# Another order of DRAM rows over the partitions in a contrast kernel

## The chip, the cores and the metric

The kernel runs on one core of a Trainium2 chip. The metric is the device time of one execution in microseconds; the median of three runs before the change is 239.33 us (239.33 to 239.63).

## The reference

The input x is float32, 16 x 3 x 512 x 512: 48 images (16 batches of 3 channels) of 262,144 pixels. Each image is stretched about its own mean, by a factor of 1.5, and clipped to [0, 1]:

```
mean = np.mean(x, axis=(2, 3), keepdims=True)
return np.clip(mean + factor * (x - mean), 0, 1).astype(np.float32)
```

So each output is factor * x plus a number that belongs to its image, (1 - factor) * mean, clipped. The mean needs the whole image before the first pixel of it can be written. 50.3 MB are read and 50.3 MB are written.

## The kernel before

**Tiles.** A row of the kernel is 16,384 consecutive elements (`ROW`, 64 KiB), an image is 16 rows (`ppi`), and a tile is 128 rows, one on each partition: eight whole images (`per_tile`). There are six tiles, 0 to 5 in the code ("tiles two to six" of a count from one are `t` = 1 to 5). `dram(ap, t, c0, c1)` gives the DRAM side of a transfer: rows 128t to 128t + 127 in order, so that row r of the tile stands on partition r, and columns c0 to c1 of each. `load` (L77) and `store` (L80) move such a piece between DRAM and one of three slots of `ring`; both are issued by SyncE, so all transfers go through its one queue in program order.

**Constants.** `blockw`, 128 x 128, holds `wconst` = (1 - factor) / 262,144 where both partitions belong to the same image (the same block of 16) and 0 elsewhere. GpSimd builds it with a memset (L61) and two selects (L63).

**One tile.** `compute(t)` first sums each partition's row. `add` splits it: VectorE reduces the first 4,352 columns (`SUM`, L85), ScalarE copies the other 12,032 in place with an accumulated sum (L89). Two matmuls with the stationary `blockw` (L100) add the two columns of sums over the partitions of an image, scale them by `wconst`, and leave the image's number on each of its partitions in a column of `bias` in PSUM. VectorE then does x * factor + bias (L103) and the clip (L106), both in place, and `store` sends the slot out. Tile 0 is loaded in three pieces, summed in two halves, and stored in two pieces (the first 2,048 columns ahead).

**Order.** The schedule is written out by hand: loads of tiles 0, 1, 2; then `compute` of 0, 1, 2 with their stores; loads of 3, 4, 5; then `compute` of 3, 4, 5. There are 15 transfers: eight loads and seven stores. The load of tile t + 3 waits until the store of tile t has emptied its slot. In the queue, that gives the loads of tiles 0 to 2, the stores of 0 to 2, the loads of 3 to 5, and the stores of 3 to 5.

Of the kernel before, what the change touches and what calls it, by code (L numbers as in the profile page):

```python
# [1 line left out]

# [4 lines left out]


P = 128  # L10
ROW = 16384
HALF = ROW // 2
BUFS = 3
SHORT = 2048
SUM = 4352


@with_exitstack
def kernel(
    ctx: ExitStack,  # L20
    tc: tile.TileContext,
    x: bass.AP,
    factor: float,
    out: bass.AP,
):

    nc = tc.nc
    f32 = mybir.dt.float32  # L30
    Alu = mybir.AluOpType
    Act = mybir.ActivationFunctionType

    B, C, H, W = x.shape
    n_img, n_pix = B * C, H * W
    ppi = n_pix // ROW
    per_tile = P // ppi
    n_tiles = n_img // per_tile
    assert ppi * ROW == n_pix and per_tile * n_tiles == n_img

    factor = float(factor)
    wconst = (1.0 - factor) / float(n_pix)

    x_f = x.rearrange("b c h w -> (b c h w)")
    out_f = out.rearrange("b c h w -> (b c h w)")

    def dram(ap, t, c0=0, c1=ROW):
        return bass.AP(tensor=ap.tensor, offset=t * P * ROW + c0, ap=[[ROW, P], [1, c1 - c0]])

    consts = ctx.enter_context(tc.tile_pool(name="consts", bufs=1))  # L50
    xpool = ctx.enter_context(tc.tile_pool(name="xpool", bufs=1))
    small = ctx.enter_context(tc.tile_pool(name="small", bufs=1))
    psum = ctx.enter_context(tc.tile_pool(name="psum", bufs=1, space=bass.MemoryType.PSUM))


    sums = small.tile([P, 4 * n_tiles], f32, name="sums")
    bias = psum.tile([P, n_tiles], f32, name="bias")

    blockw = consts.tile([P, P], f32, name="blockw")
    blocks = blockw.rearrange("p (a b) -> p a b", b=ppi)  # L60
    nc.gpsimd.memset(blockw, wconst)  # L61
    for base, step in ((0, -ppi), (ppi - 1, ppi)):
        nc.gpsimd.affine_select(  # L63
            out=blocks,
            in_=blocks,
            compare_op=Alu.is_ge,
            fill=0.0,
            base=base,
            pattern=[[step, per_tile], [0, ppi]],
            channel_multiplier=1 if step < 0 else -1,  # L70
        )


    ring = xpool.tile([P, BUFS, ROW], f32, name="ring")

    def load(t, c0=0, c1=ROW):
        nc.sync.dma_start(out=ring[:, t % BUFS, c0:c1], in_=dram(x_f, t, c0, c1))  # L77

    def store(t, c0=0, c1=ROW):
        nc.sync.dma_start(out=dram(out_f, t, c0, c1), in_=ring[:, t % BUFS, c0:c1])  # L80

    def add(t, col, c0, c1, c2):
        xt = ring[:, t % BUFS, :]
        own = sums[:, 4 * t + col : 4 * t + col + 2]
        nc.vector.tensor_reduce(  # L85
            out=own[:, 0:1], in_=xt[:, c0:c1], axis=mybir.AxisListType.X, op=Alu.add
        )
        part = xt[:, c1:c2]
        nc.scalar.activation(out=part, in_=part, func=Act.Copy, accum_out=own[:, 1:2])  # L89
        return [own[:, 1:2], own[:, 0:1]]  # L90

    def compute(t, *cuts):
        xt = ring[:, t % BUFS, :]
        if t == 0:
            parts = add(t, 0, 0, SUM, HALF) + add(t, 2, HALF, HALF + SUM, ROW)
        else:
            parts = add(t, 0, 0, SUM, ROW)
        shift = bias[:, t : t + 1]
        for k, part in enumerate(parts):
            nc.tensor.matmul(shift, blockw, part, start=k == 0, stop=k == len(parts) - 1)  # L100
        for c0, c1 in zip((0, *cuts), (*cuts, ROW)):
            part = xt[:, c0:c1]
            nc.vector.tensor_scalar(  # L103
                out=part, in0=part, scalar1=factor, scalar2=shift, op0=Alu.mult, op1=Alu.add
            )
            nc.vector.tensor_scalar(  # L106
                out=part, in0=part, scalar1=0.0, scalar2=1.0, op0=Alu.max, op1=Alu.min
            )
            store(t, c0, c1)

    with tc.manual_schedule():
        load(0, 0, SHORT)
        load(0, SHORT, HALF)
        load(0, HALF, ROW)
        load(1)
        load(2)
        compute(0, SHORT)
        compute(1)
        compute(2)
        load(3)  # L120
        load(4)
        load(5)
        compute(3)
        compute(4)
        compute(5)


# [1 line left out]
_INS = ['x', 'factor']  # L129
_OUTS = [((16, 3, 512, 512), 'float32')]  # L130

_NUMBERS = {'factor': 1.5}


# [26 lines left out]
```

## Time and profile before

| what | value |
|---|---|
| median of three runs | 239.33 us (239.33 to 239.63) |
| span of the profiled execution, first to last instruction | 237.3 us |
| the median less that span | 2.0 us |
| VectorE busy | 137.4 us in 21 instructions |
| ScalarE busy | 59.9 us in 15 |
| TensorE busy | 7.9 us in 28 |
| GpSimd busy | 1.1 us in 7 |
| x * factor + bias over a whole tile (L103), clip (L106) | 8.76 us, 8.70 us each |
| sum of a tile on VectorE (L85), on ScalarE (L89) | 4.68 us, 10.23 us |
| issue of one load or store on SyncE, median | 0.42 us, 0.34 us |

The span is made of one profiled execution; the page gives no other time of that execution, so the two microseconds between it and the median of the runs are taken to lie around the span. Engines are named as on the page: PE is TensorE, DVE is VectorE, ACT is ScalarE, POOL is GpSimd, and SPq is SyncE's queue. The page's row "DMA" has the span in 40 equal slices, and each digit is the busy share of the 16 DMA engines in tenths.

### The profile page before, as it was taken

What the parts mean: (1) busy time and instruction counts of PE and PEld (TensorE: products, weight loads), DVE (VectorE), ACT (ScalarE), POOL (GpSimd) and SP (SyncE); (2) the same over time, 40 slices, a digit from 0 to 9 for tenths busy, and PEclk for the clock granted to TensorE, in tenths of its full rate; (3) what the DMA queues carried; (4) which work ended last, traced back from release to release, by engine and by line L of the source; (5) the groups of instructions that cost most, each with busy time, mean ns of one, the idle gap of its engine ahead of it and who ended that gap; (6) DMA issues with size and microseconds to landing.
All of it is one profiled execution on the core that took longest, in us unless ns stands there. A gap on an engine that the chain in (4) does not pass through costs nothing.

```text
span 237.3 us, 186 instructions
## 1 busy us (share of the span) xinstructions
PE 7.9 (3%) x28; PEld 6.9 (3%) x28; DVE 137.4 (58%) x21; ACT 59.9 (25%) x15; POOL 1.1 (0%) x7
## 2 busy tenths in 40 slices
PE   0010100010001000000000000100000000000000
PEld 0010100010001000000000000100000000000000
DVE  0071899949998998000000043499989998991000
ACT  2051300980492000000000049319509800000000
POOL 1000000000000000000000000000000000000000
DMA  7999989899799798989899998989899998989894
GB/s 289 418 442 442 530 353 530 353 486 398 331 464 454 341 530 353 530 353 519 365 442 442 398 486 353 530 354 530 353 475 409 431 453 376 508 353 530 353 530 177
DMA packets 2160, 100.66 MB, mean 424 GB/s; under 512 B 240, under 2 KB 240, under 8 KB 240
## 3 DMA queue, kind: packets, MB, share of 16 engines
q1 hardware_dynamic: 2160, 100.66, 98.7%
HBM read 50.33 MB, written 50.33 MB: 424 GB/s over the span
## 4 chain that ended last, share of the span: by engine, by line
DVE 43%; DMA 36%; ACT 9%; PE 2%; SPq 1%; issue 0%; DVEq 0%; ACTq 0%
DMA ring<-in_x_dram 36%; DVE ring L103 18%; DVE ring L106 18%; ACT ring L89 9%; DVE sums L85 6%; PE bias L100 2%; SPq L77 1%; SPq L80 0%; DVEq L103 0%; ACTq L89 0%
## 5 line engine op out<-in xcount | busy, mean ns | idle before, releaser
L89 ACT ACTIVATE ring<-ring 128x12032 f32<-128x12032 f32 (+1 forms) x7 | 58.0, 8280 | 128.2 <-DMA ring<-in_x_dram 128.2
L85 DVE TENSOR_REDUCE sums<-ring 128x1 f32<-128x4352 f32 x7 | 32.8, 4683 | 63.9 <-DMA ring<-in_x_dram 63.9
L103 DVE TENSOR_SCALAR ring<-ring,bias 128x16384 f32<-128x16384 f32 (+2 forms) x7 | 52.8, 7538 | 12.9 <-PE bias L100 12.9
L106 DVE TENSOR_SCALAR ring<-ring 128x16384 f32<-128x16384 f32 (+2 forms) x7 | 52.3, 7476 | 0.2
L100 PE MATMUL bias<-sums,blockw 128*128 128x1 f32 x28 | 7.9, 360 | 189.1 <-ACT ring L89 175.4
L100 PEld LDWEIGHTS bias<-sums,blockw 128*128 128x128 f32 x28 | 6.9, 314 | 190.0 <-ACT ring L89 159.4
L89 ACT ACT_TABLE_LOAD x1 | 1.3, 1283 | 0.8 <-PEq L142 0.8
L89 ACT ACTIVATION_READ_ACCUMULATOR ring<-ring 128x1 f32 x7 | 1.3, 187 | 0.0
L63 POOL TENSOR_SCALAR_AFFINE_SELECT blockw<-blockw 128x128 f32<-128x128 f32 x2 | 0.7, 340 | 0.1
L61 POOL MEMSET blockw<- 128x128 f32 x1 | 0.2, 204 | 0.3 <-POOLq L142 0.3
L142 POOL MEMSET const-bfloat16-1.0<- 128x1 bf16 x1 | 0.1, 102 | 0.0
L142 POOL MEMSET const-uint8-127<- 128x1 uint8 x1 | 0.1, 102 | 0.0
L142 POOL MEMSET const-float32-0.0<- 128x1 f32 x1 | 0.1, 98 | 0.3 <-issue 0.3
L142 POOL MEMSET const-float32-1.0<- 128x1 f32 x1 | 0.1, 98 | 0.0
## 6 DMA issues: line engine op xcount, KB each, us to landing
out_dram<-ring SPq DMA_DIRECT2D x1, 7168.0 KB, 35.9
ring<-in_x_dram SPq DMA_DIRECT2D x1, 4096.0 KB, 20.8
ring<-in_x_dram SPq DMA_DIRECT2D x1, 3072.0 KB, 11.6
ring<-in_x_dram SPq DMA_DIRECT2D x1, 1024.0 KB, 4.7
out_dram<-ring SPq DMA_DIRECT2D x1, 1024.0 KB, 34.3
ring<-in_x_dram SPq DMA_DIRECT2D x5, 57.7
out_dram<-ring SPq DMA_DIRECT2D x5, 27.0
```

The costliest lines, as they stand in the source:

```text
L61: nc.gpsimd.memset(blockw, wconst)
L63: nc.gpsimd.affine_select(out=blocks, in_=blocks, compare_op=Alu.is_ge, fill=0.0, base=base, pattern=[[step, per_tile], [0, ppi]], channel ...
L77: nc.sync.dma_start(out=ring[:, t % BUFS, c0:c1], in_=dram(x_f, t, c0, c1))
L85: nc.vector.tensor_reduce(out=own[:, 0:1], in_=xt[:, c0:c1], axis=mybir.AxisListType.X, op=Alu.add)
L89: nc.scalar.activation(out=part, in_=part, func=Act.Copy, accum_out=own[:, 1:2])
L100: nc.tensor.matmul(shift, blockw, part, start=k == 0, stop=k == len(parts) - 1)
L103: nc.vector.tensor_scalar(out=part, in0=part, scalar1=factor, scalar2=shift, op0=Alu.mult, op1=Alu.add)
L106: nc.vector.tensor_scalar(out=part, in0=part, scalar1=0.0, scalar2=1.0, op0=Alu.max, op1=Alu.min)
L142: nc = _bacc.Bacc("TRN2", target_bir_lowering=False, num_devices=1)
```

## The change

For every tile but tile 0 the DRAM side of loads and stores is walked in two steps: an outer index e of 16 with a step of one row, and an inner index k of 8 with a step of 16 rows. The SBUF side is still the 128 partitions in order. So row 16k + e of the tile stands on partition 8e + k. The image of row 16k + e is k, so an image now has one partition in each block of eight, the partitions with the same remainder by 8, and needs another matrix of weights. `member`, 8 x 128, gets a 1 where partition p has the remainder j; the matmul of it with itself gives `same`, a 1 wherever two partitions have the same remainder; VectorE scales that out of PSUM into `dealtw`. Tiles 1 to 5 use `dealtw` as the stationary operand, tile 0 still uses `blockw`. Loads and stores use the same order, so each result goes back where its pixel came from.

```diff
+GROUPS = 16
...
     def dram(ap, t, c0=0, c1=ROW):
-        return bass.AP(tensor=ap.tensor, offset=t * P * ROW + c0, ap=[[ROW, P], [1, c1 - c0]])
+        rows = [[ROW, GROUPS], [GROUPS * ROW, P // GROUPS]] if t else [[ROW, P]]
+        return bass.AP(tensor=ap.tensor, offset=t * P * ROW + c0, ap=[*rows, [1, c1 - c0]])
...
+    own = P // GROUPS // per_tile
+    member = consts.tile([per_tile, P], f32, name="member")
+    groups = member.rearrange("p (a b) -> p a b", b=P // GROUPS)
+    nc.gpsimd.memset(member, 1.0)
+    for base, step in ((0, 1), (own - 1, -1)):
+        nc.gpsimd.affine_select(
+            out=groups,
+            in_=groups,
+            compare_op=Alu.is_ge,
+            fill=0.0,
+            base=base,
+            pattern=[[0, GROUPS], [step, P // GROUPS]],
+            channel_multiplier=-step * own,
+        )
+    same = psum.tile([P, P], f32, name="same")
+    dealtw = consts.tile([P, P], f32, name="dealtw")
+    nc.tensor.matmul(same, member, member, start=True, stop=True)
+    nc.vector.tensor_scalar(
+        out=dealtw, in0=same, scalar1=wconst, scalar2=None, op0=Alu.mult
+    )
...
-            nc.tensor.matmul(shift, blockw, part, start=k == 0, stop=k == len(parts) - 1)
+            nc.tensor.matmul(shift, dealtw if t else blockw, part, start=k == 0, stop=k == len(parts) - 1)
```

## The prediction, made before the result was known

> **What bounds the kernel now.** I read the page first, for its DMA part, then the waits of SyncE's queue, then the time line, and last the single packet records of the trace.
>
> ```profile
> span 237.3 us, 186 instructions
> PE 7.9 (3%) x28; PEld 6.9 (3%) x28; DVE 137.4 (58%) x21; ACT 59.9 (25%) x15; POOL 1.1 (0%) x7
> ...
> DMA  7999989899799798989899998989899998989894
> ...
> DMA packets 2160, 100.66 MB, mean 424 GB/s; under 512 B 240, under 2 KB 240, under 8 KB 240
> ...
> q1 hardware_dynamic: 2160, 100.66, 98.7%
> ```
>
> No engine is busy for more than 58% of the span, while the one DMA queue keeps 16 engines busy for 98.7% of it. The kernel issues 15 transfers (8 loads, 7 stores), and 2160 packets are 15 x 144: each transfer is 128 packets of data, one per partition, and 16 small ones that tell of its end. So a packet is one row of up to 65,536 bytes.
>
> The packet records give the price of a row. Of 1,280 packets of 65,536 bytes the median is 2.418 us, and nearly all take exactly that, loads and stores alike; the shorter rows of tile 0 take 0.309 us (8,192 bytes), 0.912 (24,576), 1.213 (32,768) and 2.116 (57,344). Each of the 16 engines carries 8 rows of every transfer: tile 0 in 8 x (0.309 + 0.912 + 1.213) = 19.47, tile 0 out 8 x (0.309 + 2.116) = 19.40, the other five tiles in and out 80 x 2.418 = 193.44, and 15 x 0.009 for the small packets: 232.45 us. The first packet starts 1.82 us into the span and the last ends at 236.08, so the transfers take 234.26. Only 1.8 us is neither start, nor end, nor a row at its own pace, and the records say where that is: 0.59 us per engine in tile 0's first rows (the first sixteen packets took 0.61 to 1.02 us for 0.309), 1.12 in the sixteen rows that start at 58.0 to 58.4 us (3.23 to 3.79 for 2.418), and 0.16 in rows around 122 and 175 us.
>
> ```profile
> 58.00:62.00 4.00, 0.00 (x0) 0.00 (x0) 4.00 (x1) 0.00 (x0) 0.00 (x0) 1.00 0.93 291
> ...
> 101.00:120.00 19.00, 0.00 (x0) 0.00 (x0) 0.00 (x0) 0.00 (x0) 0.00 (x0) 1.00 1.01 438
> ```
>
> These are windows of the busy time per engine; the last three figures are the granted clock, the DMA share and GB/s. In the first window the engines are occupied but move 291 GB/s; in the second, an undisturbed one, 438. The slow rows are the last ones of tile 2's load, just ahead of the first store. The rows at 175 us are the last ones of tile 5's load, ahead of tile 3's store. Those are the two places where the queue turns from loads to stores.
>
> ```profile
> SPq L80 <- DVE ring L106: 181.8, 7, 47.8
> SPq L77 <- DMA out_dram<-ring: 25.6, 2, 19.3
> ...
> 205.87 8.70 DVE L106 TENSOR_SCALAR ring<-ring 128x16384 f32<-128x16384 f32 x1
> ```
>
> SyncE's queue waits for VectorE and for stores, but the DMA engines do not run dry meanwhile, since earlier transfers stand in the queue. The thinnest cover is at the end: VectorE is done at 214.57 us and the last store is issued then, while tile 4's store lands at 216.5 to 217.1: about 2 us. The chain of waits runs through VectorE there, but what sets the time is the queue beside it.
>
> **The change, part by part.**
>
> *Setup, added.* POOL gets one memset and two selects on 8 partitions. By the rows for the same on 128 partitions (0.204 and 2 x 0.340) that is at most 0.9 us behind the 1.82 where POOL ends now: 2.7. TensorE then multiplies 8x128 by 8x128; no row has 128 moving columns in float32. Below it is a pair of bias matmuls (0.59 us on the time line), above I allow four of these: 2.4. VectorE scales 128x128 out of PSUM; the bounds are 0 and the 1.29 us of its 128x2048 operation. So the new weights are there by 2.7 + 2.4 + 1.3 = 6.4 us at the latest. The added waits are two. VectorE waits for the matmul, and behind it stands its first sum, at 12.94 (it waits for the load); the matmul that waits for that sum starts after it. TensorE waits for POOL, and behind it stands the first bias matmul, at 16.50. Cost 0 with over 6 us to spare; without that cover it would be up to 4.6 us on tile 0's first sum.
>
> *Bias matmuls.* The same 28 passes with another stationary operand of the same shape: 0.
>
> *DMA issue.* Still 15 instructions; the DRAM side gets one dimension more for ten of them. An issue takes 0.42 us (loads) or 0.34 (stores) at the median. If the longer pattern doubled this, tiles 1 and 2 would be issued at most 1 us later than the 3.3 us at which that ends now, and they are due at 22 us; at the end 0.34 of the 2 us goes. Between 0 and that, all hidden: 0.
>
> *The rows themselves.* Same bytes, same number, same length, the same partitions in all; what moves is which DRAM row stands on which partition. If eight neighbouring partitions belong to one engine, the 16 engines now read 16 neighbouring rows at a time, where before each read rows of its own block. Before shows only the old order, so I bound it. From below: the 1.28 us in the slow long rows is all that an order of rows could give back, since every other row of these tiles runs at one pace, the same for reading and for writing, whatever its address. From above: two engines that get in each other's way all the time would double 80 rows, + 193.4 us. I take 0. The nearest row is the 2.418 itself: it is the same to the nanosecond over hundreds of rows in six tiles and two tensors, which is how a limit of the engine looks and not one of memory. And the 1.12 us sits at a turn from loads to stores, not with any row of tiles 0 and 1 at the same place in their blocks; the turn stays, with an undealt store behind it.
>
> [...]
>
> *Sum.* 0 + 0 + 0 + 0: the profiled span stays 237.3. The runs take 239.33 (median), 2.0 us more, which lies around the span. Forecast **239.3**, with 238.9 to 239.8 as its own range (0.2% is 0.48 us, about what a measurement of this kernel can tell from no change).
>
> **The rivals.**
>
> *The slow rows vanish (faster).* If the long rows at 58 and 175 us are slow because of their addresses, the new order may free them: 237.3 - 1.12 to - 1.28, so about 238.1. For it: sixteen rows of one transfer, all slow together. Against it: only where the direction turns. A part of it, over 0.5 us, would already count as faster.
>
> *Two engines share a way into SBUF (much slower).* The old pattern has 128 rows in its outermost dimension on both sides, the new one 16 on the DRAM side. Whoever cuts the transfer into 16 shares may then have to cut blocks of eight partitions where it had another cut before. If these blocks meet in pairs at the same place in SBUF, a row takes up to 2 x 2.418 = 4.836 us: 80 x 2.418 = + 193 us, about 432; pairs that drift apart would lose less. It decides from 6 ns a row (0.5 us over 80 rows). For it: 27.1 GB/s per engine on every row means that today no two engines meet, so the present cut is one that avoids it. Against it: nothing in the trace says that the cut follows the dimension, or that blocks of eight meet.
>
> [...]
>
> *Neighbouring rows disturb one another (slower).* 1 to 3% on a row that sixteen engines now read or write side by side is 80 x 0.024 to 0.073 = + 1.9 to + 5.8: 241 to 245. For it: the first sixteen packets of the run, all starting together, took two to three times their pace. Against it: after those two rows of packets the same engines ran at one pace, still in step within 0.4 us.
>
> *The setup is late (slower).* Over 6 us of cover; + 1 to 4 us if POOL or TensorE take far longer than their rows.
>
> **How the numbers follow.** No change 0.33; slow rows vanish 0.29; neighbours disturb 0.18; shared way 0.18; late setup 0.02. The likeliest is 239.3. Faster is the second case and a sliver of the first, 0.30; within 0.2% 0.32; slower the rest, 0.38. The range reaches to 237.9 for the freed rows and to 246 for disturbed neighbours and a late setup; only the shared way, 0.18, and slivers lie outside.
>
> **What would show it.** The page after should have 2160 packets, 98 to 99% on the queue, 424 GB/s, and a first VectorE sum still at 12.9 us; the weights' VectorE operation ends before 6.4. The window 58 to 62 us tells the first rival: over 400 GB/s there, and the span shrinks by 1.1. The shared way would show in tile 1's load, the first dealt one: it lands at 41.9 now and would land near 61. Disturbed neighbours would show as a mean rate a few per cent below 424 with no idle DMA. The prediction is wrong if a dealt row doesn't take 2.418 us, or if the slow rows at 58 us were theirs and not the turn's.

## The result and the profile after

The changed kernel takes **427.13 us** (median of five runs, 423.78 to 428.29) against 239.33: a ratio of 1.782, 95% interval 1.776 to 1.789. Forecast was 239.3 with a range of 237.9 to 246. The time is that of the rival "two engines share a way into SBUF", which had been worked out as about 432 and given a chance of 0.18.

The page of the changed kernel answers to the lines shown of before. First the span and the engines' busy time, then the rows of 40 equal slices, then the packets and the queue:

```profile
span 422.1 us, 193 instructions
PE 8.2 (2%) x30; PEld 7.1 (2%) x30; DVE 138.1 (33%) x22; ACT 59.9 (14%) x15; POOL 1.9 (0%) x10
...
DMA  8999999999999899999999999999999999998951
GB/s 353 442 230 267 199 199 199 199 199 286 429 378 199 199 199 248 230 217 230 205 217 211 211 205 224 199 211 217 211 242 298 267 248 248 273 255 248 248 155 43
DMA packets 2160, 100.66 MB, mean 239 GB/s; under 512 B 240, under 2 KB 240, under 8 KB 240
...
q1 hardware_dynamic: 2160, 100.66, 96.8%
```

The engines do the work they did before. There are as many packets with as many bytes, and the 16 DMA engines are still busy nearly all the time, 96.8%. Only the rate has fallen, from 424 to 239 GB/s. So no engine waits for work to be issued; the packets themselves are slow. The row "GB/s" also shows where: two stretches run at or near the old rate, the first two slices and the eleventh and twelfth. Those are tile 0's load and tile 0's store, the tile that keeps the old pattern. The slices of tile 1's and tile 2's loads, the fifth to the ninth, stand at 199, less than half of 424.

The packet records say it by rows. Rows of tile 0 keep their median times to the nanosecond (0.309, 0.912, 1.213 and 2.116 us). Of the 1,280 rows of 65,536 bytes, which nearly all took 2.418 before (mean 2.434), the median is now 4.998 us and the mean 4.608; tile 1's load starts with rows of 4.5 to 4.8 and goes on at 4.9 to 5.1. Per engine that is 80 x (4.608 - 2.434) = 174 us of the 184.8 by which the span grew. The rest is the end: the sixteen engines finish the last store between 401.3 and 420.9 us, where they had finished within 0.6 us of each other.

The time line shows the new weights, and the first work on a dealt tile:

```profile
2.57 0.79 PE L92 MATMUL same<-member 8*128 8x128 f32 x2 [2.57 <-POOL member L81]
3.40 0.29 DVE L93 TENSOR_SCALAR dealtw<-same 128x128 f32<-128x128 f32 x1 [3.40 <-PE same L92]
...
12.88 4.69 DVE L109 TENSOR_REDUCE sums<-ring 128x1 f32<-128x4352 f32 x1 [9.18 <-DMA ring<-in_x_dram]
...
63.41 10.23 ACT L113 ACTIVATE ring<-ring 128x12032 f32<-128x12032 f32 x1 [36.99 <-DMA ring<-in_x_dram]
```

Before, the same two places stood so:

```profile
12.94 4.69 DVE L85 TENSOR_REDUCE sums<-ring 128x1 f32<-128x4352 f32 x1 [12.94 <-DMA ring<-in_x_dram]
...
41.93 10.23 ACT L89 ACTIVATE ring<-ring 128x12032 f32<-128x12032 f32 x1 [15.86 <-DMA ring<-in_x_dram]
```

The weights are ready at 3.69 us and VectorE's first sum starts at 12.88, where it was 12.94: the setup costs nothing. Tile 1, the first dealt one, is there at 63.41 us instead of 41.93. Counted from the end of tile 0's load, it takes 40.5 us instead of 19.4.

In the waits, VectorE and ScalarE now stand for loads for 171.7 and 269.1 us. The first two lines are of before, the last two of the changed kernel (us in total, times, longest):

```profile
ACT ring L89 <- DMA ring<-in_x_dram: 128.2, 7, 67.2
DVE sums L85 <- DMA ring<-in_x_dram: 63.9, 3, 46.0
...
ACT ring L113 <- DMA ring<-in_x_dram: 269.1, 7, 127.1
DVE sums L109 <- DMA ring<-in_x_dram: 171.7, 7, 108.3
```

### The profile page after: what moved, and what is told of

The parts are those of the page before. It is cut to its first block, busy times and chain, and to the rows that moved or that the text cites. A ratio compares the mean times of both kernels' runs of the same rounds, so it can differ in the third digit from the quotient of the medians.

```text
span 422.1 us, 193 instructions
## 1 busy us (share of the span) xinstructions
PE 8.2 (2%) x30; PEld 7.1 (2%) x30; DVE 138.1 (33%) x22; ACT 59.9 (14%) x15; POOL 1.9 (0%) x10
## 3 DMA queue, kind: packets, MB, share of 16 engines
q1 hardware_dynamic: 2160, 100.66, 96.8%
## 4 chain that ended last, share of the span: by engine, by line
another core or an unknown queue 60%; ACT 13%; DMA 5%; DVE 4%; PE 0%; SPq 0%; issue 0%; ACTq 0%; DVEq 0%
ACT ring L113 13%; DMA ring<-in_x_dram 5%; DVE ring L127 2%; DVE ring L130 2%; PE bias L124 0%; SPq L101 0%; ACTq L180 0%; ACTq L113 0%; DVEq L127 0%
## 5 line engine op out<-in xcount | busy, mean ns | idle before, releaser
L113 ACT ACTIVATE ring<-ring 128x12032 f32<-128x12032 f32 (+1 forms) x7 | 58.0, 8279 | 269.1 <-DMA ring<-in_x_dram 269.1
L109 DVE TENSOR_REDUCE sums<-ring 128x1 f32<-128x4352 f32 x7 | 32.8, 4686 | 171.7 <-DMA ring<-in_x_dram 171.7
L124 PE MATMUL bias<-sums,dealtw 128*128 128x1 f32 x20 | 5.1, 357 | 297.5 <-ACT ring L113 297.5
L124 PEld LDWEIGHTS bias<-sums,dealtw 128*128 128x128 f32 x20 | 4.6, 322 | 297.9 <-ACT ring L113 297.9
L124 PE MATMUL bias<-sums,blockw 128*128 128x1 f32 x8 | 2.3, 362 | 22.5 <-ACT ring L113 21.3
L124 PEld LDWEIGHTS bias<-sums,blockw 128*128 128x128 f32 x8 | 2.0, 311 | 23.1 <-ACT ring L113 21.6
```

Source lines behind the costliest of these rows:

```text
L109: nc.vector.tensor_reduce(out=own[:, 0:1], in_=xt[:, c0:c1], axis=mybir.AxisListType.X, op=Alu.add)
L124: nc.tensor.matmul(shift, dealtw if t else blockw, part, start=k == 0, stop=k == len(parts) - 1)
```

## The experiments

Three theories went in. **A**: with 16 outermost on the DRAM side, each engine's share is a block of eight neighbouring partitions, and the engines then meet in pairs at groups of partitions that let only one row's worth through. **B**: it is the DRAM order, sixteen neighbouring rows at a time. **C**: any further dimension in the pattern slows a transfer.

### One cause at a time

**e1_mirror8** keeps every block of rows on its own partitions and only walks it backwards, so that the pattern is 16 x 8 while the DRAM neighbourhood is that of before. The weights are those of before, since a block lies within one image.

```diff
-        return bass.AP(tensor=ap.tensor, offset=t * P * ROW + c0, ap=[[ROW, P], [1, c1 - c0]])
+        rows, first = [[ROW, P]], 0
+        if t:
+            rows, first = [[8 * ROW, 16], [-ROW, 8]], 7 * ROW
+        return bass.AP(tensor=ap.tensor, offset=t * P * ROW + first + c0, ap=[*rows, [1, c1 - c0]])
```

> The kernel before, but tiles 1 to 5 write the DRAM side as 16 blocks of 8 rows, each block walked backwards (row 8e+7-k on partition 8e+k). Every block of rows stays on its own eight partitions, so the DRAM neighbourhood is that of before; only the outermost count goes from 128 to 16. Theory A (16 outermost makes an engine's share eight neighbouring partitions, and pairs of engines then share a way into SBUF): about 427 us, rows of 65,536 bytes at about 5.0 us. Theory B (it is the DRAM order, sixteen neighbouring rows at a time): 239 us, rows at 2.42. Theory C (any further dimension in the pattern slows a transfer): about 427.

**e1b_three_dims** leaves 128 outermost and adds a dimension further in.

```diff
+        if t:
+            return bass.AP(tensor=ap.tensor, offset=t * P * ROW + HALF, ap=[[ROW, P], [-HALF, 2], [1, HALF]])
```

> The kernel before, but tiles 1 to 5 have their two halves of columns swapped between DRAM and SBUF: three dimensions on both sides, 128 outermost on both, pieces of 32,768 bytes. Theory A: 239 us, pieces at 1.21 us. Theory C: far slower, towards 427. Theory B: 239.

**e2_near_chunks** has 128 outermost, too, and puts the pieces of neighbouring partitions side by side in DRAM.

```diff
+        if t:
+            return bass.AP(tensor=ap.tensor, offset=t * P * ROW, ap=[[4096, P], [128 * 4096, 4], [1, 4096]])
```

> The kernel before, but in tiles 1 to 5 partition p holds the four chunks of 16,384 bytes p, p+128, p+256 and p+384 of the tile: 128 outermost, and what the engines read at one time lies together within 2 MB, with chunks of neighbouring partitions side by side. A partition then holds pieces of four images, so the means of tiles 1 to 5 are not the reference's. Theory B (DRAM neighbours disturb one another): clearly slower, up to 427 us. Theory A: 239 us within 1%, 16,384 bytes at about 0.61 us. Theory C: slower.

**e3_deal32** is the changed kernel with one count changed and the weights to match (`member` has a 1 where 2 x (p mod 4) + p // 64 is j).

```diff
-GROUPS = 16
+GROUPS = 32
```

> The changed kernel with 32 instead of 16 outermost: row 32k+a on partition 4a+k, weights to match. Theory A, if the share is always a block of eight neighbouring partitions: about 427 us as with 16. [...] Theory B: slow, near 427, since sixteen engines still read side by side. Theory C: slow.

| run | median, us | ratio to before, 95% interval | rows in tiles 1 to 5 |
|---|---|---|---|
| e1_mirror8 | 425.88 | 1.777 (1.769 to 1.785) | 65,536 bytes: median 4.961 us |
| e1b_three_dims | 239.56 | 0.999 (0.998 to 1.001) | 32,768 bytes: 1.213 |
| e2_near_chunks | 240.14 | 1.003 (1.002 to 1.004) | 16,384 bytes: 0.611 |
| e3_deal32 | 239.39 | 1.000 (0.998 to 1.001) | 65,536 bytes: 2.418 |

The first run has none of the new DRAM order, none of the new weights, and the loss all the same: 1.777 against 1.782. The second takes C away. The third speaks against B: pieces that lie together cost 0.3%, with 6,000 packets instead of 2,160. The fourth settles B, as far as a run can: by the author's estimate sixteen engines still read rows out of one neighbourhood (no record names the row of a packet), the second matrix of weights is there, and the loss is gone. Of theory A it leaves the form in which the outermost count decides: 4.961 us a row under 16 in e1_mirror8, 2.418 under 32. The packet lines of e1_mirror8 and then of e3_deal32, in that order:

```profile
DMA packets 2160, 100.66 MB, mean 237 GB/s; under 512 B 240, under 2 KB 240, under 8 KB 240
...
q1 hardware_dynamic: 2160, 100.66, 96.4%
```

```profile
DMA packets 2160, 100.66 MB, mean 424 GB/s; under 512 B 240, under 2 KB 240, under 8 KB 240
...
q1 hardware_dynamic: 2160, 100.66, 98.6%
```

The two have the same packets and bytes and keep the queue nearly equally busy, but not the same rate. Between e3_deal32 and the changed kernel (96.8%, 239 GB/s) only the outermost count of the pattern differs, 32 or 16, with what follows from it: which row stands on which partition, and the weights.

The same run answers the rival "the slow rows vanish". Here is the window at the first turn from loads to stores, and one later, in e3_deal32 (the last three figures are granted clock, DMA share and GB/s):

```profile
58.00:62.00 4.00, 0.00 (x0) 0.00 (x0) 4.00 (x1) 0.00 (x0) 0.00 (x0) 1.00 0.87 256
101.00:120.00 19.00, 0.00 (x0) 0.00 (x0) 0.00 (x0) 0.00 (x0) 0.00 (x0) 1.00 0.99 428
```

The dip is still there at 256 GB/s (291 before) with another row on each partition. So it is not tied to the order of rows that before had. No faster version came out of it: dealt over 32 the kernel is as fast as before, not faster.

### The partitions that share

**e4_halves** uses the old row order and two dimensions, but sends the partitions in two transfers.

```diff
+    def cuts(t):
+        return ((0, 64), (64, P)) if t else ((0, P),)
...
+        for p0, p1 in cuts(t):
+            nc.sync.dma_start(out=ring[p0:p1, t % BUFS, c0:c1], in_=dram(x_f, t, c0, c1, p0, p1))
```

(`store` likewise.)

> The kernel before, but each transfer of tiles 1 to 5 is made as two, of partitions 0 to 63 and 64 to 127, rows in the old order, two dimensions only. [...] A theory in which only the 16-outermost pattern is at fault: about 240 us (ten more issues, hidden).

422.76 us, ratio 1.766 (1.738 to 1.795), rows at a median of 5.06 us:

```profile
DMA packets 2320, 100.66 MB, mean 237 GB/s; under 512 B 400, under 2 KB 400, under 8 KB 400
...
q1 hardware_dynamic: 2320, 100.66, 95.8%
```

So the loss needs no 16-row pattern at all; transfers of one half of the partitions are enough. That the sixteen engines then crowd into this half is theory A's reading. This run alone does not exclude that transfers of fewer rows are slow in themselves; the next one does.

**e10_probe** measures the groups by themselves: each transfer alone, a few rows of 65,536 bytes, the partitions chosen. In its code `rows(first, step, n)` names them.

```diff
+        nc.sync.dma_start(out=rows(0, 1, 2), in_=src(2))
+        settle()
...
+        nc.sync.dma_start(out=dst(8), in_=rows(0, 4, 8))
```

> No adjustment of contrast: after one tile's load, 17 loads of 2 to 16 rows of 65,536 bytes into chosen partitions, each alone, then six stores of 2 or 8 rows, then six stores of a tile; the output is not the reference's. Theory A, with groups of four neighbouring partitions and p with p + 32 in one group, and one engine for each row: two rows on partitions 0 and 1, 0 and 2, or 0 and 32 take about 5.0 us each; on 0 and 4, 0 and 8, 0 and 16, 0 and 64, 0 and 96 about 2.42. Four rows on 0 to 3: about 10; on 0, 4, 8, 12: 2.42; on 0, 32, 64, 96: 5.0. Eight rows on 0 to 7: about 10; on 0, 4, ... 28: 2.42; on 0, 16, ... 112: 5.0. Sixteen rows on 0 to 15: about 10; on 0, 4, ... 60: 5.0. Twelve on 48, 52, ... 92: 2.42. Stores the same. If partitions have nothing to do with it, all rows take 2.42.

The time line of SyncE's queue in e10_probe shows the start of each issue. Each store waits until the one before it has landed and VectorE has touched the tile, so the step from one line to the next is the price of a transfer. L136 to L156 are stores of partitions 0 and 1; 0 and 4; 0 and 32; 0 and 64; 0 to 7; and 0, 4, ... 28. L80 is the next store.

```profile
146.06 0.26 SPq L136 DMA_DIRECT2D out_dram<-ring  x1
152.54 0.68 SPq L140 DMA_DIRECT2D out_dram<-ring  x1
156.94 0.51 SPq L144 DMA_DIRECT2D out_dram<-ring  x1
163.83 0.50 SPq L148 DMA_DIRECT2D out_dram<-ring  x1
168.04 0.29 SPq L152 DMA_DIRECT2D out_dram<-ring  x1
179.72 0.70 SPq L156 DMA_DIRECT2D out_dram<-ring  x1
184.22 0.37 SPq L80 DMA_DIRECT2D out_dram<-ring  x1
```

The steps are 6.5, 4.4, 6.9, 4.2, 11.7 and 4.5 us. Two rows cost 2.1 us more on partitions 0 and 1 than on 0 and 4, and 2.7 more on 0 and 32 than on 0 and 64; eight rows cost 7.2 more side by side than four apart. The records of the rows themselves:

| rows on partitions | load, us a row | store, us a row |
|---|---|---|
| 0, 1 | 3.95 to 4.12 | 5.07 to 5.09 |
| 0, 2 | 4.26 to 4.50 | |
| 0, 32 | 4.09 to 4.73 | 5.07 to 5.09 |
| 0, 4; 0, 8; 0, 16; 0, 64; 0, 96 | 2.77 to 3.60 | 2.45 (0, 4 and 0, 64) |
| 0, 1, 2, 3 | 7.75 to 9.01 | |
| 0, 4, 8, 12 | 3.21 to 3.59 | |
| 0, 32, 64, 96 | 3.94 to 4.88 | |
| 0 to 7 | 7.33 to 9.03 | 9.86 to 10.18 |
| 0, 4, ... 28 | 2.47 to 3.32 | 2.45 to 2.46 |
| 0, 16, ... 112 | 4.27 to 4.99 | |
| 0 to 15 | 7.31 to 9.23 | |
| 0, 4, ... 60 | 4.35 to 5.25 | |
| 48, 52, ... 92 | 2.42 to 3.32 | |

The stores are as expected within 0.2 us. The loads keep the expected order, but not the numbers: rows that share with none take up to 1.2 us over 2.418, and shared ones are up to 27% under what was expected. Why is open. As far as they were tried, neighbours within 0 to 3, and partitions 32 apart, are in one group, and partitions 4, 8, 16, 64 or 96 apart are not. In the stores a row takes 2.45 us alone in its group, 5.08 with one other, 10 with three others.

### Loads or stores

> The kernel with mirrored blocks of eight, for loads alone; the stores of tiles 1 to 5 have the old pattern, so their rows land in mirrored order within blocks of eight. Theory A with a way into SBUF that is shared by writing and by reading alike: half of the extra time, 427 - 239 = 188 over two, so about 333 us, with 640 rows at about 5.0 us and 640 at 2.42. If it is the writing into SBUF alone: 427. If it is the reading alone: 239.

**e7_mirror_loads** has the 16 x 8 pattern for loads alone: 343.54 us, ratio 1.435 (1.431 to 1.440), 10 us over the 333 expected. **e8_mirror_stores** has it for stores alone.

```diff
-        nc.sync.dma_start(out=dram(out_f, t, c0, c1), in_=ring[:, t % BUFS, c0:c1])
+        nc.sync.dma_start(out=dram(out_f, t, c0, c1, True), in_=ring[:, t % BUFS, c0:c1])
```

(`dram` takes the mirrored rows where its last argument is true.)

> The kernel with mirrored blocks of eight, for stores alone; the loads of tiles 1 to 5 have the old pattern, so their rows land in mirrored order within blocks of eight. With loads alone mirrored the run took 343.5 us, 104 of the 187 that both cost. Theory A with reading and writing sharing alike: the other 84, about 323 us, and up to 343 if stores meet as often as loads. Only writing into SBUF is hurt: 239.

326.06 us, 1.362 (1.358 to 1.366). Loads alone add 104 us, stores alone 87, together 191; both at once, in e1_mirror8, added 186. Both directions are slowed. That stores lose less goes with engines that drift apart, though no run isolates it: in e8_mirror_stores the engines end the last store 12.6 us apart, and some of its mirrored rows still take 2.42 us. In each mirrored load of the other run the engines stay in step and end within 1.6 us of each other.

### Engines out of step

If two engines meet because they walk through their blocks in step, a lead of four rows should part them. **e5_stagger4** and **e6_stagger12and4** put useless loads of 4 or 12 rows ahead of tile 1, meant to hold up fewer than 16 engines. That the partners are engines four apart in number is the author's assumption: it would follow from the probe's groups (stores of partitions 0 and 32 took 5.07 to 5.09 us a row) if engine e carried partitions 8e to 8e + 7, which no record shows.

```diff
         load(0, HALF, ROW)
+        for base, n in [(0, 4), (4, 4), (8, 4), (12, 4)]:
+            nc.sync.dma_start(
+                out=ring[base : base + n, 2, :],
+                in_=bass.AP(tensor=x_f.tensor, offset=base * ROW, ap=[[ROW, n], [1, ROW]]),
+            )
         load(1)
```

(e6_stagger12and4: four of 12 rows, then four of 4.)

> The changed kernel with four useless loads of 4 rows each ahead of tile 1's load, into the slot that tile 2 fills later. If a transfer of 4 rows goes to 4 engines, one row each, these four are now four rows behind. Theory A with pairs of engines four apart in number: the pairs with one late engine no longer meet, so half of the rows of 65,536 bytes come at about 2.42 us and half at about 5.0; the total stays near 427, since the other half of the engines is as slow as before. Theory A with other pairs, or a loss that does not come from pairs: nearly all rows stay at about 5.0 us.

> The changed kernel with eight useless loads ahead of tile 1's load: four of 12 rows, then four of 4 rows. If they go to the 12 and the 4 engines of lowest number, engines 0 to 3 are eight rows late, 4 to 7 four, 8 to 11 four and 12 to 15 none: every pair four apart is out of step. Theory A with such pairs: 64 rows more to read, and yet faster than the changed kernel by some 90 to 150 us, 270 to 340 us; rows mostly at about 2.42 us. Any other theory: 427 plus up to 19.

Both missed. e5_stagger4 took 434.78 and 446.98 us in its two runs, e6_stagger12and4 447.95 and 452.35. The useless rows had been put on neighbouring partitions and crowded each other, four to a group: 64 rows of e5_stagger4 took 9.1 to 11.8 us. Only 16 rows were useless ones; the other 48 belong to tile 1's load, which was in flight beside them, twelve rows at a time. By e10_probe partitions 0 to 3 are in one group, and 0 with 32; if a group is four neighbours and the four that lie 32 above them, which is an estimate from these sets, not all twelve can have gone to the crowded one. So by this estimate a crowded group held up engines with work elsewhere, too.

The crowd does not explain the whole miss of e5_stagger4. After it, from 62.5 to 117 us, the four late engines were, by the count of rows, four rows behind the other twelve: 16 rows of 65,536 bytes were still to be read when the others had gone on to tile 0's store. Half of the engines were to run at 2.42 us a row then. But every row took 4.8 to 5.6 us, and the rate was that of the changed kernel, 208 GB/s:

```profile
64.00:104.00 40.00, 0.00 (x0) 0.00 (x0) 0.00 (x0) 0.00 (x0) 0.00 (x0) 1.00 1.00 208
```

So either the partners are not engines four apart, or two that meet slow down all the loads in flight, and not only each other. No run separates the two.

Tile 2's load in e6_stagger12and4 did go faster than the same load in the changed kernel, where it takes 40.4 us. Windows of e6_stagger12and4, first with the crowd, then in tile 2's load:

```profile
35.00:100.00 65.00, 0.00 (x0) 0.00 (x0) 12.15 (x2) 0.00 (x0) 0.00 (x0) 1.00 0.97 113
103.00:129.00 26.00, 0.00 (x0) 0.00 (x0) 2.67 (x1) 2.67 (x1) 0.00 (x0) 1.00 0.99 313
```

The first is 113 GB/s, about a quarter of 424, as if all engines went at the pace of four to a group; the second is 313, with the dealt pattern unchanged. In that load the rows go by fours, for instance 4.6, 3.8, 2.42, 2.43 us and then the same again. Theory A reads this as an engine that meets another for part of four rows and is free for the rest. All sixteen engines are fast or slow together: the sixteen rows in flight at 107.5 us take 2.42 to 2.43, those at 113.5 us 4.3 to 4.9.

**e9_stagger_clean** puts the useless rows on partitions four apart.

```diff
+        extra = [(48 + i, 12) for i in range(4)] + [(i, 4) for i in range(4)]
+        for first, n in extra:
+            nc.sync.dma_start(
+                out=ring[first : first + 4 * n - 3 : 4, 2, :],
+                in_=bass.AP(tensor=x_f.tensor, offset=first * ROW, ap=[[ROW, n], [1, ROW]]),
+            )
```

> The changed kernel with the eight useless loads of 12 and 4 rows again, but on partitions four apart (48, 52, ... 92 and 0, 4, 8, 12, then shifted by one), so that they should not meet among themselves. Theory A with groups of four partitions and pairs of engines four apart: the useless rows take about 2.42 us each, and tile 1's load, with each pair three to four rows out of step, takes 20 to 28 us in place of 40.5; the total falls below the changed kernel's 427 in spite of 64 rows more, 290 to 380 us. If rows are slow whenever 16 is outermost, in step or not: 427 to 446 us and 5.0 us a row.

Half of it came. The first 24 of the 64 useless rows took 2.42 to 2.48 us, so they were slow before for their partitions alone. But tile 1's load was as slow as ever. The two runs took 413.91 and 420.87 us; both lie below all five of the changed kernel, in spite of 64 rows more, but 1.7% apart they do not say by how much, and 290 to 380 had been expected.

Tile 1's first rows did not start until 28 us, 6 us after tile 0's had ended; they are taken to be on the four engines without useless rows. Where the others were is read from the rows that follow each other end to start: eight began tile 1 at about 34.5 us, only 1.3 rows later, so most of their lead was gone; the last four were at useless rows until about 55. All rows that started between 29 and 64 us took 4.8 to 5.1 us, useless ones, too, so here as well four engines that lagged brought nothing. Tile 2's load had a little: windows of e9_stagger_clean over most of tile 1's load and of tile 2's (the trace is that of the longer run),

```profile
30.00:68.00 38.00, 0.00 (x0) 0.00 (x0) 16.13 (x3) 0.00 (x0) 0.00 (x0) 1.00 0.96 205
70.00:102.00 32.00, 1.02 (x4) 0.93 (x4) 5.74 (x2) 10.32 (x2) 0.00 (x0) 1.00 0.96 232
```

205 and 232 GB/s, and most of the rows that follow each other end to start go by fours again: 4.5, 5.1, 4.5, 2.42. That an offset can help is shown by these two loads, by that of e6_stagger12and4 above all. That the partners are engines four apart in number is not, since the trace does not name the engine of a packet.

## Why the prediction was wrong

**The step that failed** is "The rows themselves": of the bounds from - 1.28 to + 193.4 us it took 0, because "the nearest row is the 2.418 itself". That row did not speak to the question. It was measured under the old pattern, with all 16 engines at one even pace, and so it said that the old order was harmless, but nothing of what another pattern does. The runs showed 4.608 us a row in the mean in its place (2.434 before), and a ragged end. The upper bound was the right price: 187.8 us were lost against 193.4 worked out. Its parts were a little off in both directions. A shared row took mostly 4.9 to 5.1 us rather than 4.836, as in the probe's stores, where two rows of one group take 5.08; and engines drifted apart in the later stores, where some rows took 2.42 again.

The spacing of the rows in DRAM was not the cause. Row 16k + e stands on partition 8e + k, so within a block of eight, neighbouring partitions hold rows 16 apart, 1 MiB, where before it was one row, 64 KiB. But e1_mirror8 keeps neighbours 64 KiB apart and is as slow (4.961 us a row), while e3_deal32 has them 2 MiB apart within its blocks of four and takes 2.418 us a row.

**Shared way, 0.18.** By its time and its sign it was the case. "The old pattern has 128 rows in its outermost dimension on both sides, the new one 16" is the very edit that e1_mirror8 isolates. What was held against it, that nothing in the trace says that blocks of eight meet, was only silence of the trace, and it outweighed the reason that stood beside the rival, the even pace of 27.1 GB/s per engine. The sign named for it came: tile 1's load was to land near 61 us and landed at 63.4. The rival's 432 us are 1% from what was measured. What the runs show of the sharing itself is e10_probe: a stored row takes 2.45 us alone in its group and 5.08 with one other. That pairs of engines share in this way is inferred.

**No change, 0.33, for the DRAM side.** Right about DRAM: e3_deal32 shows the dealt rows at 2.418 us. **Neighbours disturb, 0.18.** Not seen there, and 0.3% (0.2 to 0.4) in e2_near_chunks, which has more packets, too. **Slow rows vanish, 0.29.** Wrong: the dip at the turn stays in e3_deal32. **Setup, bias matmuls, issue.** Right, each 0: the weights came at 3.69 us for 6.4 at the latest, the matmul took 0.79 of an allowed 2.4 and VectorE's scaling 0.29 of 1.29.

**What stays open.** That the share of an engine is a block of eight neighbours under 16 outermost is inferred: with the probe's groups it explains the 4.961 us a row of e1_mirror8, but no record names the partition of a packet. What the share is under 32 or 128, where a row took 2.418 us, was not shown. Which engines meet is open, and so is why all sixteen are slow together where by theory A only some of them meet.

## What to carry to other kernels

The transfers of this kernel kept the DMA engines 96.8% busy and yet ran at 239 GB/s, against 424 at 98.7% before: compare bytes per second with busy share, and look at the time of one packet (4.998 us at the median against 2.418). When rows are dealt to partitions in blocks, it is the outermost count of the pattern that matters here: 16 blocks of eight cost 78%, 32 blocks of four nothing that could be measured (ratio 1.000). And a duration that is constant in the old trace bounds only what the old arrangement exercised; where an edit changes the arrangement, the far bound deserves the weight that the reasons for it have.

## What the runs showed of the hardware that was not expected

A crowd slowed rows of another transfer beside it: in e5_stagger4, 48 rows of tile 1's load took 9.1 to 11.8 us beside 16 useless rows that were four to a group, and by the estimate above not all of them can have gone to the crowded group. After that crowd all sixteen engines stayed slow, at 208 GB/s, although by the count of rows four of them were four rows behind; and in e6_stagger12and4 all sixteen were fast or slow at the same time (2.42 to 2.43 us a row at 107.5 us, 4.3 to 4.9 at 113.5). Two rows in one group cost more than twice one: 5.08 us each for stores against 2.45 alone. And the dip at the turn from loads to stores (256 GB/s for four microseconds in e3_deal32) is there in both orders of rows that were looked at (291 in before); its cause was not looked for.
